# Weight blocks brought forward in a two-block mixer kernel, and the buffers rearranged for them

## The chip, the cores and the metric

The kernel runs on one core of a Trainium2 chip, as one program. The metric is the device time of an execution in microseconds. Three runs of the kernel before took 1659.3, 1660.58 and 1669.26 us; the median, 1660.58 us, is the time before.

## The reference, cut to what matters

Two blocks work on 256 latent tokens (and 256 context tokens in the first block) of width 1024, in float32. The first block has two layers:

```python
# layer 0 (context and latents), then layer 1 (latents only at the end)
mod = silu(c) @ mod_w[layer] + mod_b[layer]           # six vectors of 1024: sh1, sc1, g1, sh2, sc2, g2
h   = rmsnorm(x, norm_mix_g) * (1 + sc1) + sh1
y   = even_mixer(h)  (layer 0)   or   odd_mixer(h)  (layer 1)
x   = x + g1 * y
h   = rmsnorm(x, norm_ffn_g) * (1 + sc2) + sh2
x   = x + g2 * (silu(conv(h @ w_up)_g) * conv(h @ w_up)_a) @ w_down
```

`even_mixer` is a gated linear attention (4 heads) and an mLSTM (4 heads), both in two directions; their eight head outputs, 128 features each, go through `even_w_out` (1024 x 1024). `odd_mixer` is an SSD with 4 groups of 8 heads in two directions; the group outputs of 512 features are gated by silu(z), normalised per group and go through `ssd_w_out` (2048 x 1024). `w_up` is 1024 x 5632. The second block (attention, recurrence and gating branches) is not touched by the change.

## The kernel before, in words

Activations are kept with features on the 128 partitions. Every large weight is loaded as float32 in blocks of mostly 128 x 2048 (1 MB) and split in two halves of 16 bits: `get_w` (L318) asks SP for the load into a staging tile `st`, ScalarE casts it to `whi` (float16), and VectorE or GpSimd (`eng`) writes the rest, `wlo` = `st` - `whi` (bfloat16). A product then takes three matmuls per 128 x 128 weight tile, `whi` by the high half of the activations, `whi` by the low half, `wlo` by the high half (`proj_fm`, L328). The common staging pool `wst` and the common pool of halves `wsp` have three buffers each; `pool` and `parts` put the staging tile or the halves elsewhere.

The order of instructions on each engine isn't written out by hand: the program is traced in the order of the Python code, and a planner, which simulates the engines as it goes, places the instructions, earlier code first, later code where an engine would be free. What it placed runs in that order on every engine. A tile of a pool that reuses memory waits for the tiles that lay there.

- `layer0_mixer` (L538): gated linear attention, mLSTM inputs, the mLSTM heads one after another (`hd` 0 to 3, each ends with `hm` and is split into `h`). Then the tail: mod steps 2, 3 and 4 of layer 0 (`mod_steps`, four loads of 1 MB each, multiplied in float32 straight from staging), the four blocks of `even_o` (blocks 0 and 1 take the first four head outputs, 2 and 3 the last four), the products `eo` with their residual additions into `xT`, the norm of the context tokens and mod step 5. The blocks' halves are in the pool `tw` of four buffers. The products and the mod steps share two accumulators (`mm`).
- `ffn` (L972), called for layer 0 with both streams and for layer 1 with the latents. The 22 w_up blocks have their low part on GpSimd, those of odd number a staging pool of their own (`stage`). During the first FFN, the mod steps of layer 1 run as halves of 0.5 MB with pools `ms` and `mp` of two buffers, one half after each w_up block and the rest inside the down projection.
- `ssd` (L1083): for each group g, `inputs(g + 1)` is traced between the heads of group g (`heads`), and the output product of an earlier group (`out`) beside it; `take` advances these generators. `steps` prepares the decays once, with softplus. The output of the heads of all four groups is in `ys`, 16 tiles of 128 x 256 in two halves. For group 3 the scale `factor` is applied after the product: `ps` is multiplied by it (`so`) before the residual additions. In `out`, group g reads `ys` from 4g. At the end of `ssd` w_up blocks 0 and 1 of the second FFN are traced (`first_up`), in the common pools.
- `ffn` for layer 1 then norms the latents (`rstd_bc`: squares, a chain of additions `sq`, `rsqrt`; then `nt`, `hh`, `hl` per 128 features) and goes on with these two blocks.

Of the kernel before, what the change touches and what calls it, by code (L numbers as in the profile page):

```python
# [10 lines left out]
F32 = mybir.dt.float32  # L11
# [237 lines left out]
class Program:  # L249
# [288 lines left out]
    def layer0_mixer(self):  # L538
        h, I = self.h, self.I
        with ExitStack() as ph:  # L540
            gp = self.pool("gp", 1, None, ph)
            ev = self.pool("ev", 1, None, ph)
            mp = self.pool("mp", 1, None, ph)
            yf = ev.tile([128, 8, 512], F32, name="yf")
            mqk = ev.tile([128, 8, 512], F32, name="mqk")
            vext = ev.tile([128, 4, 4, 129], F32, name="vext")
            self.rows = [mp.tile([128, 512], F32, name=n) for n in ("li", "lf", "lb", "lm")]
            for t in self.rows:
                self.G.memset(t[:64], 0.0)
            self.G.memset(vext[:, :, :, 128:129], 1.0)  # L550
            self.gla(gp, h, I["even_w"], yf)
            self.mlstm_inputs(h, I["even_w"], mqk, vext, yf)
            for i in range(4):
                self.split(h[0][:, i], h[1][:, i], yf[:, i])
            self.mlstm(mp, h, mqk, vext, yf)
            self.dbg("ym", h[0])
        self.res2 = self.pool("res2")
        self.xT = self.res2.tile([128, 8, 512], F32, name="xT")
        self.nc.sync.dma_start(self.xT, I["xT"].rearrange("p (k t) -> p k t", k=8))
        with ExitStack() as tail:  # L560
            tw = self.pool("tw", 4, None, tail)
            for r in (2, 3, 4):
                for _ in self.mod_steps(0, r, whole=True):
                    pass
            w = [self.get_w(I["even_o"][b], 4, 512, parts=tw) for b in range(4)]

            for b in range(2):
                for c in range(4):
                    ps = self.mm("eo")
                    self.proj_fm(ps, w[b], c * 128, 128, h, 0, 512, nk=4)  # L570
                    self.add_residual(ps, 0, 2, 4 * b + c, BOTH)

            for s in range(2):
                for b in range(2):
                    for c2 in range(2):
                        ps = self.mm("eo")
                        for c in range(2):
                            self.proj_fm(ps[:, c * 256:c * 256 + 256], w[2 + b], (2 * c2 + c) * 128, 128, h,
                                         256 * s, 256 * s + 256, nk=4, h0=4)
                        for c in range(2):  # L580
                            self.add_residual(ps[:, c * 256:], 0, 2, 4 * b + 2 * c2 + c, ((s, 0, 256),), 256 * s)
                if s == 0:
                    self.norm_stream(0, 1, 0, "ml")
            for _ in self.mod_steps(0, 5, pool=tw, whole=True):
                pass
        self.dbg("xmid0", self.xT)
# [385 lines left out]
    def ffn(self, l, streams):  # L972
        I, V = self.I, self.V
        both = len(streams) == 2
        n, t0 = (512, 0) if both else (256, 256)
# [3 lines left out]
        if both:  # L979
# [3 lines left out]
            for i in range(3):  # L983
                w = self.get_w(I["w_up"][l, i], 8, 256, self.G)
# [21 lines left out]
        with ExitStack() as ph:  # L1006
            fp = self.pool("fp", 1, None, ph)
            f2 = self.pool("f2", 3, None, ph)
            stage = self.pool("stage", 1 if both else 3, None, ph)
# [1 line left out]
            self.nc.sync.dma_start(fcw, I["fcw"][l].rearrange("p (c j) -> p c j", c=44))  # L1011
            hid = self.pair(fp, "hid", [128, 22, n])
            if both:
                ms, mp = self.pool("ms", 2, None, ph), self.pool("mp", 2, None, ph)
                up = True
                mods = chain.from_iterable(self.mod_steps(1, r, eng=lambda: self.G if up else None, pool=ms, parts=mp,
                                                          halves=True) for r in range(6))
            for i in range(22):
                begun = both and i < 3
                if begun:  # L1020
                    w, pss = first[i]
                elif not both and i < 2:
                    w = self.first_up[i]
                else:
                    w = self.get_w(I["w_up"][l, i], 8, 256, self.G, (None, stage)[i % 2])
                us = []
                for c in range(2):
                    ps = pss[c] if begun else self.mm("up")
# [43 lines left out]

    def layer1_mixer(self):
        h, I = self.h, self.I
        with ExitStack() as ph:
            sp = self.pool("sp", 1, None, ph)
            s2 = self.pool("s2", 2, None, ph)
            y = self.pair(sp, "ys", [128, 16, 256])
            self.ssd(sp, s2, h, y)
            self.dbg("ys", y[0])  # L1080
        self.dbg("xmid1", self.xT[:, :, 256:512])

    def ssd(self, sp, s2, h, y):  # L1083
# [17 lines left out]
        def steps(ps):  # L1101


            t1 = lambda n: sp.tile([128, 256], F32, name=n)
            z, e, u, q, dt, cum = t1("z"), t1("e"), t1("u"), t1("q"), t1("dt"), t1("cum")
            self.ts(z, ps[:, :256], self.pp("sdtb"), op0=ALU.add)
            self.softplus(dt, z, e, u, q, 256)
            self.dbg("dt", dt)
# [58 lines left out]
        def out(g, factor=None):  # L1167

            for b in range(2):
                w = self.get_w(I["ssd_o"][2 * g + b], 4, 512)  # L1170
                for c in range(2):
                    ps = self.mm("so")
                    for cc in range(2):
                        self.proj_fm(ps[:, cc * 256:cc * 256 + 256], w, c * 256 + cc * 128, 128, y, 0, 256, nk=4, h0=4 * g)
                    if factor is not None:
                        t = s2.tile([128, 512], F32, tag="xs", name="so")
                        self.tt(t.rearrange("p (c t) -> p c t", c=2), ps.rearrange("p (c t) -> p c t", c=2), bc(factor, 1, 2), ALU.mult)
                        ps = t
# [18 lines left out]
        def inputs(g, d):  # L1197
# [32 lines left out]
            px = self.ps("fr", "bTT")  # L1230
            for t in range(4):
                T.transpose(px[:, t * 128:t * 128 + 128], bT[:, t * 128:t * 128 + 128], self.ident)
            bt = d["bt"] = s2.tile([128, 4, 128], F32, tag="bt", name="bt")
            self.act(bt, px.rearrange("p (a b) -> p a b", a=4))
            ps = self.ps("fr", "CB")
            for sb in range(2):
# [43 lines left out]
        def heads(g, D):  # L1280
# [3 lines left out]
            for j in range(4):  # L1284
# [41 lines left out]
                                 start=True, stop=True)  # L1326
                self.tt(yt[:, j], yt[:, j], Y[:, :256], ALU.add)
                self.tt(yt[:, j], yt[:, j], D["sz"][:, j], ALU.mult)
                sq = s2.tile([128, 256], F32, tag="ssq", name="ssq", bufs=4)
                self.act(sq, yt[:, j], AF.Square)  # L1330
                if j:
                    self.tt(sq, sq, sums, ALU.add)
                sums = sq
                if g == 3:
                    self.split(y[0][:, 12 + j], y[1][:, 12 + j], yt[:, j], scale=hg[:, 12 + j:13 + j])
            ps = self.ps("fr", "ss")
            for tb in range(2):
                T.matmul(ps[:, tb:tb + 1], sums[:, tb * 128:tb * 128 + 128], self.ones[:, 0:1], start=True, stop=True)
# [1 line left out]
            r = self.cols.tile([128, 2], F32, tag="sr", name="sr")  # L1340
            self.ts(v, ps[:, 0:2], 1.0 / 2048, EPS, ALU.mult, ALU.add)
            self.rsqrt(r, v, 2)
            dg = s2.tile([128, 2, 128], F32, tag="dg", name="dg")
            self.tt(dg, bc(self.ident, 1, 2), bc(r, 2, 128), ALU.mult)
            yield
            pb = self.ps("fr", "rb")
# [5 lines left out]
            for j in range(4):  # L1352
                k = 4 * g + j
                self.stt(yt[:, j], yt[:, j], hg[:, k:k + 1], pb[:, :256], ALU.mult, ALU.mult)
                self.split(y[0][:, k], y[1][:, k], yt[:, j])

        def take(it, n=1):
            for _ in range(n):
# [5 lines left out]
        for g in range(4):  # L1364
# [16 lines left out]
            take(now)  # L1381
            if g < 3:
                states(g + 1, nxt)
                nxt["factor"] = None
                D = nxt
            else:
                factor = D["factor"]
        take(out(3, factor), 99)

        self.first_up = [self.get_w(I["w_up"][1, i], 8, 256) for i in range(2)]  # L1390

    def softplus(self, o, z, e, u, q, n):

# [536 lines left out]
    def run(self):  # L1930
# [31 lines left out]
        self.layer1_mixer()  # L1962
        self.set_psum(mm=7, nb=1)
        self.ffn(1, ((1, 0, 256),))
        self.dbg("xend1", self.xT[:, :, 256:512])
        self.set_psum(mm=2, pT=1, av=1, x=1, sc=2, fl=1)
        self.block2()
# [27 lines left out]
```

## Time and profile before

| | |
|---|---|
| median of the runs | 1660.58 us (1659.3 to 1669.26) |
| the profiled execution | 1671.3 us, its span 1669.5 us |
| TensorE busy | 1579.9 us (95%) |
| VectorE busy | 1205.0 us (72%) |
| ScalarE busy | 848.8 us (51%) |
| GpSimd busy | 449.1 us (27%) |
| granted TensorE clock, mean | 0.972 |
| HBM read | 233.68 MB, 141 GB/s over the span |

Times in views of the trace are microseconds from the start of the span. PE is TensorE, PEld its weight loads, DVE VectorE, ACT ScalarE, POOL GpSimd, SP the engine that issues the loads (its rows show the issue, not the transfer). A row of the timeline gives start, duration, engine, line of the kernel (often that of a helper), operation, output and inputs, count, and in brackets the idle time of the engine before it with what ended it. The stages: first mixer to about 360, first FFN to 740, SSD to 1071, second FFN to 1270, then the second block.

### The profile page before, as it was taken

How to read it: one execution, taken by the hardware profiler on the slowest of the kernel's cores; microseconds unless marked ns; L12 is line 12 of the kernel's file. 1: busy time of each engine (PE TensorE's matmuls, PEld its weight loads, DVE VectorE, ACT ScalarE, POOL GpSimd, SP SyncE). 2: the span in 40 equal slices, each digit the busy share in tenths (PEclk: the TensorE clock that was granted, in tenths of full speed). 3: DMA queues.
4: the chain of work that ended last, by engine and by line, in shares of the span. 5: the costliest groups of instructions: out<-in, count | busy, mean ns of one | idle time of the engine just before them, and what ended most of it. 6: DMA issues, size and time to landing. Idle time of an engine off the chain costs nothing.

```text
span 1669.5 us, 31742 instructions
## 1 busy us (share of the span) xinstructions
PE 1579.9 (95%) x12913; PEld 1088.6 (65%) x12978; DVE 1205.0 (72%) x2636; ACT 848.8 (51%) x1390; POOL 449.1 (27%) x265
## 2 busy tenths in 40 slices
PE   6999999899999999998999999599999999999988
PEld 3566865477444444375566667488887887778877
DVE  6888745778777786556878888799967875366734
ACT  4746424435545544434566564366664644556532
POOL 0000000035878730000000000079944212421240
PEclk9999999899999999999999999799999989999999
DMA  9322126633443346632222323335454343433641
GB/s 388 106 80 77 53 77 255 262 145 114 152 151 126 119 160 211 200 115 76 101 76 77 126 76 131 153 132 201 150 184 163 139 164 107 147 114 124 231 158 51
DMA packets 41186, 236.77 MB, mean 142 GB/s; under 512 B 4688, under 2 KB 5456, under 8 KB 21200
## 3 DMA queue, kind: packets, MB, share of 16 engines
q1 hardware_dynamic: 41040, 234.74, 39.9%
q8 instruction: 102, 1.67, 0.4%
q14 instruction: 44, 0.36, 0.1%
HBM read 233.68 MB, written 1.05 MB: 141 GB/s over the span
## 4 chain that ended last, share of the span: by engine, by line
PE 75%; DVE 11%; ACT 5%; DMA 4%; issue 4%; POOL 1%; ACTq 0%; SPq 0%; DVEq 0%; POOLq 0%
PE up L332 18%; PE dn L332 5%; PE sx L332 5%; PE fm L332 4%; PE mg L332 4%; DVE wlo L294 3%; ACT whi L306 3%; DVE u L303 3%; PE br L332 3%; PE tm L339 3%; PE eo L332 2%; PE so L332 2%; PE sz L332 2%; DMA st<-in_mod_w_dram 2%; PE mod L505 2%
## 5 line engine op out<-in xcount | busy, mean ns | idle before, releaser
L332 PEld LDWEIGHTS <-whi 128*128 128x128 f16 (+2 forms) x5240 | 512.7, 99 | 259.4 <-issue 36.9
L294 POOL TENSOR_TENSOR wlo<-st,whi 128x1024 bf16<-128x1024 f32 (+2 forms) x102 | 315.2, 3102 | 964.4 <-ACT whi L306 651.8
L306 ACT ACTIVATE whi<-st 128x2048 f16<-128x2048 f32 (+3 forms) x242 | 370.0, 1538 | 266.4 <-PE up L332 45.4
L294 DVE TENSOR_TENSOR wlo<-st,whi 128x2048 bf16<-128x2048 f32 (+3 forms) x140 | 278.9, 1997 | 93.7 <-ACT whi L306 89.1
L332 PEld LDWEIGHTS <-wlo 128*128 128x128 bf16 (+2 forms) x2620 | 259.9, 99 | 125.9 <-issue 12.4
L303 DVE SCALAR_TENSOR_TENSOR u<-up,fcw,u 128x189 f32<-128x189 f32 (+3 forms) x792 | 297.8, 435 | 51.1 <-ACT u L306 42.8
L332 PE MATMUL up<-hh,whi 128*128 128x256 f16 (+1 forms) x752 | 238.5, 319 | 1.9 <-ACT hh L306 1.1
L332 PE MATMUL up<-hh,wlo 128*128 128x256 f16 (+1 forms) x752 | 238.3, 318 | 1.0
L332 PE MATMUL up<-hl,whi 128*128 128x256 bf16 (+1 forms) x733 | 231.2, 316 | 0.0
L332 PE MATMUL dn<-hidh,wlo 128*128 128x256 f16 (+1 forms) x396 | 122.4, 311 | 3.5 <-DVE wlo L294 2.7
L332 PE MATMUL dn<-hidh,whi 128*128 128x256 f16 (+1 forms) x396 | 122.3, 310 | 0.9 <-ACT whi L306 0.7
L332 PE MATMUL dn<-hidl,whi 128*128 128x256 bf16 (+1 forms) x384 | 117.8, 308 | 0.0
L306 ACT ACTIVATE u<-up,ppt,fcw 128x512 f32<-128x512 f32 (+1 forms) x88 | 57.9, 659 | 43.9 <-PE up L332 43.9
L332 PE MATMUL fm<-hh,whi 128*128 128x256 f16 x288 | 78.5, 273 | 0.5 <-DVE xc L303 0.5
L332 PE MATMUL fm<-hh,wlo 128*128 128x256 f16 x288 | 78.5, 273 | 0.0
L332 PE MATMUL fm<-hl,whi 128*128 128x256 bf16 x288 | 78.5, 273 | 0.0
L332 PE MATMUL mg<-hh,wlo 128*128 128x256 f16 x256 | 72.2, 282 | 3.1 <-POOL wlo L294 3.1
L332 PE MATMUL mg<-hh,whi 128*128 128x256 f16 x256 | 71.8, 282 | 2.1 <-ACT whi L306 1.2
L332 PE MATMUL mg<-hl,whi 128*128 128x256 bf16 x256 | 72.1, 282 | 1.2 <-DVE hl L303 1.2
L339 PEld LDWEIGHTS <-hh 128*128 128x128 f16 x640 | 62.9, 101 | 10.2 <-issue 1.1
L298 POOL TENSOR_SCALAR E<-E,rs 128x128 f32<-128x128 f32 (+1 forms) x48 | 37.1, 787 | 111.6 <-DVE rs L1669 51.1
L332 PE MATMUL sx<-hh,wlo 128*128 128x512 f16 (+1 forms) x160 | 53.3, 336 | 0.4
(539 smaller groups left out, 3043.6 us busy)
## 6 DMA issues: line engine op xcount, KB each, us to landing
st<-in_w_up_dram SPq DMA_DIRECT2D x44, 1024.0 KB, 4.9
st<-in_w_dram SPq DMA_DIRECT2D x25, 1024.0 KB, 4.8
st<-in_mod_w_dram SPq DMA_DIRECT2D x48, 512.0 KB, 4.6
st<-in_w_dn_dram SPq DMA_DIRECT2D x32, 704.0 KB, 4.1
st<-in_ssd_w_dram SPq DMA_DIRECT2D x20, 1024.0 KB, 4.9
st<-in_mod_w_dram SPq DMA_DIRECT2D x16, 1024.0 KB, 5.7
st<-in_w_m_dram SPq DMA_DIRECT2D x32, 512.0 KB, 4.4
st<-in_even_w_dram SPq DMA_DIRECT2D x14, 1024.0 KB, 4.9
```

The costliest lines, as they stand in the source:

```text
L294: (eng or self.V).tensor_tensor(o, a, b, op=op)
L298: (eng or self.V).tensor_scalar(o, a, s1, None, op0=op0)
L303: self.V.scalar_tensor_tensor(o, a, s, b, op0=op0, op1=op1)
L306: self.S.activation(o, i, func, **kw)
L332: self.T.matmul(ps, w[a][:, k, c0:c0 + cw], h[b][:, h0 + k, t0:t1], start=first and k == 0 and i == 0, stop=last and k == nk - 1 and i == 2)
L339: self.T.matmul(ps, h[b][:, k, t0:t0 + 128], w[a][:, k, c0:c0 + cw], start=k == 0 and i == 0, stop=k == nk - 1 and i == 2)
L505: T.matmul(ps[32 * j:32 * j + 32, :256], c[:, 2 * b + k], w[:, 0 if halves else k, 256 * j:256 * j + 256], start=b == k == i == 0, stop=b ...
```

## The change

It moves loads and splits, gives some of them other buffers, and makes room for these buffers.

- Layer 0 tail: `even_o` blocks 0 and 1 are traced ahead of the mod steps, in the common pools; blocks 2 and 3 stay behind them in `tw`, which has two buffers now. Mod step 5, which stages in `tw`, has two buffers too.
- First FFN: three buffers for the mod halves.
- Second FFN: block 2's low part goes to VectorE; GpSimd has it from block 3 on.
- Blocks 0 and 1 of the second FFN have halves in a pool `fu` of their own, and are traced after the states of group 3, ahead of group 3's heads, its remaining inputs and the last two output products. `fu` lives until the second FFN is over.
- For the 16 KB of `fu`: `ys` has 8 tiles (groups g and g + 2 share), softplus's z, e, u, q lie in the buffers of `E` and `wx`, `bt` and `dg` have one buffer, `ssq` three.

```diff
@@ layer0_mixer
-            tw = self.pool("tw", 4, None, tail)
+            tw = self.pool("tw", 2, None, tail)
+            w = [self.get_w(I["even_o"][b], 4, 512) for b in range(2)]
             for r in (2, 3, 4):
                 for _ in self.mod_steps(0, r, whole=True):
                     pass
-            w = [self.get_w(I["even_o"][b], 4, 512, parts=tw) for b in range(4)]
+            w += [self.get_w(I["even_o"][b], 4, 512, parts=tw) for b in (2, 3)]
@@ ffn
-                ms, mp = self.pool("ms", 2, None, ph), self.pool("mp", 2, None, ph)
+                ms, mp = self.pool("ms", 3, None, ph), self.pool("mp", 3, None, ph)
...
-                    w = self.get_w(I["w_up"][l, i], 8, 256, self.G, (None, stage)[i % 2])
+                    w = self.get_w(I["w_up"][l, i], 8, 256, self.G if both or i > 2 else None, (None, stage)[i % 2])
@@ layer1_mixer
+        self.fu_stack = self.ctx.enter_context(ExitStack())
         with ExitStack() as ph:
+            self.fu = self.pool("fu", 2, None, self.fu_stack)
...
-            y = self.pair(sp, "ys", [128, 16, 256])
+            y = self.pair(sp, "ys", [128, 8, 256])
@@ ssd
-            z, e, u, q, dt, cum = t1("z"), t1("e"), t1("u"), t1("q"), t1("dt"), t1("cum")
+            dt, cum = t1("dt"), t1("cum")
+            z, e, u, q = [s2.tile([128, 512], F32, tag=n, name=n)[:, 256 * i:256 * i + 256] for n in ("E", "wx") for i in (0,)
+                          for _ in range(2)]
...
-                        self.proj_fm(ps[:, cc * 256:cc * 256 + 256], w, c * 256 + cc * 128, 128, y, 0, 256, nk=4, h0=4 * g)
+                        self.proj_fm(ps[:, cc * 256:cc * 256 + 256], w, c * 256 + cc * 128, 128, y, 0, 256, nk=4, h0=4 * g % 8)
...
-            bt = d["bt"] = s2.tile([128, 4, 128], F32, tag="bt", name="bt")
+            bt = d["bt"] = s2.tile([128, 4, 128], F32, tag="bt", name="bt", bufs=1)
...
-                sq = s2.tile([128, 256], F32, tag="ssq", name="ssq", bufs=4)
+                sq = s2.tile([128, 256], F32, tag="ssq", name="ssq", bufs=3)
...
-                    self.split(y[0][:, 12 + j], y[1][:, 12 + j], yt[:, j], scale=hg[:, 12 + j:13 + j])
+                    self.split(y[0][:, 4 + j], y[1][:, 4 + j], yt[:, j], scale=hg[:, 12 + j:13 + j])
...
-            dg = s2.tile([128, 2, 128], F32, tag="dg", name="dg")
+            dg = s2.tile([128, 2, 128], F32, tag="dg", name="dg", bufs=1)
...
-                self.split(y[0][:, k], y[1][:, k], yt[:, j])
+                self.split(y[0][:, k % 8], y[1][:, k % 8], yt[:, j])
...
             if g < 3:
                 states(g + 1, nxt)
-                nxt["factor"] = None
                 D = nxt
-            else:
+            if g == 2:
+                self.first_up = [self.get_w(I["w_up"][1, i], 8, 256, parts=self.fu) for i in range(2)]
+            if g == 3:
                 factor = D["factor"]
         take(out(3, factor), 99)
-
-        self.first_up = [self.get_w(I["w_up"][1, i], 8, 256) for i in range(2)]
@@ run
         self.ffn(1, ((1, 0, 256),))
+        self.fu_stack.close()
```

## Rows read from the trace of the kernel before

**Rows 1.** The profile's busy times: us, share of the span, instructions.

```profile
PE 1579.9 (95%) x12913; PEld 1088.6 (65%) x12978; DVE 1205.0 (72%) x2636; ACT 848.8 (51%) x1390; POOL 449.1 (27%) x265
```

**Rows 2.** Windows: length, each engine's busy us (count), clock, DMA share, GB/s.

```profile
225.00:255.00 30.00, 29.79 (x152) 14.38 (x151) 14.72 (x41) 7.78 (x19) 0.00 (x0) 1.00 0.10 35
300.00:311.00 11.00, 7.61 (x42) 7.07 (x40) 7.29 (x33) 3.61 (x11) 0.00 (x0) 0.69 0.01 1
311.00:315.30 4.30, 0.98 (x3) 0.31 (x4) 3.98 (x10) 4.30 (x4) 0.00 (x0) 0.84 0.87 295
315.30:328.30 13.00, 12.95 (x49) 5.66 (x51) 8.91 (x18) 3.33 (x3) 0.00 (x0) 0.79 1.01 422
```

**Rows 3.** SP's timeline, end of the first mixer.

```profile
250.81 28.58 SPq L315 DMA_DIRECT2D st<-in_mod_w_dram  x9
282.58 13.53 SPq L315 DMA_DIRECT2D st<-in_even_o_dram  x3
```

**Rows 4.** Timeline of ScalarE and VectorE, end of the first mixer.

```profile
311.08 5.50 ACT L306 ACTIVATE whi<-st 128x2048 f16<-128x2048 f32 x3
313.00 2.29 DVE L294 TENSOR_TENSOR wlo<-st,whi 128x2048 bf16<-128x2048 f32 x1
```

**Rows 5.** Windows, one stretch in the first FFN's down projection.

```profile
660.00:700.00 40.00, 38.24 (x235) 15.93 (x240) 22.50 (x25) 17.86 (x19) 0.00 (x0) 1.00 0.65 208
```

**Rows 6.** Windows, end of the SSD to the second FFN.

```profile
1033.00:1084.00 51.00, 30.45 (x205) 23.25 (x204) 39.07 (x87) 15.97 (x32) 4.06 (x1) 0.78 0.40 149
```

**Rows 7.** ScalarE's timeline, end of the SSD.

```profile
1037.31 1.91 ACT L306 ACTIVATE whi<-st 128x2048 f16<-128x2048 f32 x1 [5.28 <-issue]
1057.89 1.91 ACT L306 ACTIVATE whi<-st 128x2048 f16<-128x2048 f32 x1 [3.83 <-issue]
1059.71 0.37 ACT L306 ACTIVATE factor<-rb 128x256 f32<-128x256 f32 x1
```

**Rows 8.** Timeline of TensorE and VectorE around factor.

```profile
1057.75 0.67 PE L1347 MATMUL rb<-dg,ones 128*128 128x256 f32 x2
1059.83 2.29 DVE L294 TENSOR_TENSOR wlo<-st,whi 128x2048 bf16<-128x2048 f32 x1 [2.17 <-ACT whi L306]
1062.04 1.28 DVE L294 TENSOR_TENSOR so<-so,factor 128x512 f32<-128x512 f32 x2
1062.78 0.40 PE L332 MATMUL so<-ysh,whi 128*128 128x256 f16 x1 [4.37 <-DVE so L294]
```

**Rows 9.** The tile sq (ns: min, median, max); GpSimd's timeline; the norm.

```profile
L294 DVE TENSOR_TENSOR sq<-sq,s x7: 418/426/4078, 1064.8 to 1077.2; 128x256 f32<-128x256 f32 x7
...
1072.79 4.06 POOL L294 TENSOR_TENSOR wlo<-st,whi 128x2048 bf16<-128x2048 f32 x1 [448.44 <-ACT whi L306]
```

**Rows 10.** SP's timeline, SSD to second FFN.

```profile
984.62 26.79 SPq L315 DMA_DIRECT2D st<-in_ssd_o_dram  x4
1017.20 45.29 SPq L315 DMA_DIRECT2D st<-in_w_up_dram  x5
1070.90 0.33 SPq L1011 DMA_DIRECT2D fcw<-in_fcw_dram  x1
```

**Rows 11.** Windows, two stretches in the SSD.

```profile
945.00:960.00 15.00, 14.95 (x79) 8.05 (x78) 13.16 (x26) 6.11 (x12) 0.00 (x0) 1.00 0.40 140
985.00:1000.00 15.00, 14.95 (x125) 11.06 (x125) 14.06 (x30) 9.40 (x19) 0.00 (x0) 1.00 0.41 141
```

**Rows 12.** The chain of waits (start, us); ScalarE's timeline; SSD.

```profile
994.77 2.73 PE so L332 x24
...
1043.84 0.49 ACT L306 ACTIVATE ysh<-yt,hsg 128x256 f16<-128x256 f32 x1
```

**Rows 13.** The tile bt: ns min, median, max; first and last start.

```profile
L306 ACT ACTIVATE bt<-bTT x2: 597/624/652, 944.6 to 1010.6; 128x512 f32<-128x512 f32 x2
```

**Rows 14.** The profile's loads: count, KB each, us to landing.

```profile
st<-in_w_up_dram SPq DMA_DIRECT2D x44, 1024.0 KB, 4.9
```

**Rows 15.** The tile hl in the norm before the second FFN.

```profile
L303 DVE SCALAR_TENSOR_TENSOR hl<-nt,modc,hh x8: 482/484/485, 1084.0 to 1090.0; 128x256 bf16<-128x256 f32 x8
```

## The prediction

> **What bounds the kernel now.** I read the busy times first: TensorE is busy 1579.9 us of a span of 1669.5, so some 90 us are all that better order can win, less what a higher clock gives [rows 1]. Then I took windows over each stage that the diff touches, to see where those 90 us lie, and the queues and timelines inside the windows that had idle time.
>
> The first place is the end of the first mixer. TensorE is full from 225 to 255, but from 300 to 315.3 it idles 3.39 and 3.32 us, and the granted clock falls to 0.69 there and is still 0.79 up to 328.3: for part of that time it stands at the lower of its two levels (1.2 of 2.4 GHz) after the idle time [rows 2]. What ends the idleness is a weight split. The output blocks are queued behind the mod blocks [rows 3], and their casts sit in ScalarE's queue behind the last head's work: three casts begin at 311.08, the low part of the first follows at 313.00, though three of the blocks were asked for by 296 [rows 4].
>
> The second place is the end of the down projection of the first FFN. The chain of waits names mod-weight loads there, but TensorE is busy 38.24 of 40 us [rows 5]: the chain names a cover, not a bound.
>
> The third is the end of the SSD: from 1033 to 1084 TensorE is busy 30.45 of 51 us at a granted clock of 0.78 [rows 6]. ScalarE has two casts there (1037.31 and 1057.89) for which it first stood still 5.28 and 3.83 us, and `factor`, ready to be copied, comes out behind the second at 1059.71 [rows 7]. VectorE does the low part (2.29 us), only then the multiplication by `factor` at 1062.04, and TensorE, which waited 4.37 us, goes on at 1062.78 [rows 8]. Last, the norm before the second FFN: one addition `sq` takes 4.078 us instead of 0.418, while GpSimd has the low part of the third w_up block (1072.79, 4.06 us) [rows 9].
>
> To know which cast is which I counted loads: four ssd_o, then five w_up (blocks 0, 1, 2, 4, 6), then the staged ones [rows 10]. With three weight slots, the casts at 1037.31 and 1057.89 and the one in front of GpSimd's split at 1072.79 are w_up 0, 1 and 2; each waited until the block three earlier had left its slot.
>
> **The change, part by part.** The sum is made against the profiled execution, 1671.3 us with a span of 1669.5; the median of the runs is 1660.58, 10.7 us below it. I carry the difference over to the median unchanged.
>
> *Output blocks 0 and 1 first (A).* Two 1 MB loads pass twelve mod loads on SP's queue. DMA is nearly free from 225 to 255 (share 0.10), so the mods lose nothing [rows 2]. The two splits (ScalarE 2 x 1.8, VectorE 2 x 2.29) move from 311 into that stretch, where VectorE is busy 14.72 of 30 us and ScalarE 7.78: hidden; without that cover they'd cost 8.2. The matmuls of these blocks need only the first half of the mixer's output, which is ready, so they can fill TensorE's holes. Lower end: 0, if the planner still places them after the last head. Upper end: 3.39 + 3.32 us of idle time, and 13.0 x 0.21 = 2.7 us for the clock, 9.4 together. I take **8.0**: nearer the upper end, since TensorE has nothing else to do in these holes; the 1.4 left is my estimate for accumulators, of which there are two, waiting for their residual additions. The last mod step of layer 0 has two buffers instead of four, and two of its loads wait for its first matmuls; its result is wanted only by the down projection, past 600, so 0. The first w_up splits of the first FFN now need slots that blocks 0 and 1 hold: 0, as these are gone before the norm; without that cover 4.06 us, one GpSimd split [rows 9].
>
> *Three buffers for the mod halves (B).* Ends: 0, and the idle 40 - 38.24 = 1.76 us [rows 5]. I take **0.5**, since most of the stretch is matmuls back to back.
>
> *w_up 0 and 1 in slots of their own, split during the SSD (C1).* Two loads now pass sw18, sw19 and four ssd_o loads on SP. Their splits, 2 x 1.91 and 2 x 2.29, go to about 945 to 1000; TensorE is full there, VectorE at 13.16 and 14.06 of 15 us [rows 11]. I cost them 0 under TensorE; if VectorE sets the pace they cost 4.6. At the old place the second cast vanishes in front of `factor`: VectorE could multiply about when `factor` could be out, and the stretch from TensorE's last `so` to 1062.78 loses one cast and what it holds up. Without cast and low part, `factor` waits only for its matmul (1057.75 and 0.67) and takes 0.37 itself: some 1058.9 with the handovers, instead of the 1062.04 at which VectorE could multiply, **3.1 us** won [rows 7, 8]. Ends: 0 (another cast takes the place; more than one has no free slot) and 3.83 (the whole stall). The first cast (1037.31) I price at 0: w_up 2 inherits its slot and place, with its split on VectorE as that of w_up 0 was. If nothing took its place, 2.3 more.
>
> *w_up 2's low part on VectorE (C2).* GpSimd's 4.06 us at 1072.79 go, and with them the 4.078 - 0.418 = 3.66 us that `sq` stood [rows 9]. But GpSimd keeps blocks 3 and up, and w_up 4, loaded early through the common staging, can be cast as soon as a slot is free, at the end of the SSD, where w_up 2's was. Ends: +3.66 and, if blocks 3 and 4 both hit the norm, -3.66. I take **0**: w_up 4 is loaded and the third slot comes free at the same moment as before.
>
> *Room made for it.* y of two groups: the first write for group 3 comes at 1043.84, the matmuls of out(1), which read the reused half, are over by 997.5 (994.77 and 2.73) [rows 12]: 0. One bt: the copy at 1010.6 waits for state matmuls of the group before, and that group's own copy was at 944.6, so there are 66 us between [rows 13]: 0. One dg, three ssq, and softplus's four temporaries inside E and wx come in program order after their last readers: 0 each; if ScalarE did wait for one, the P and E casts queue behind it, by at most one such copy of 0.65 us a group. The fcw load and the FFN's buffers lie 16 KB higher; staged loads still go after 1070.9 [rows 10]: 0. The second FFN is not touched inside and moves as a block.
>
> Sum: 8.0 + 0.5 + 3.1 + 0 = **11.6 us faster**: 1659.7 for a run like the profiled one, 1649.0 at the median.
>
> **The port of VectorE and GpSimd.** The row shows it: 4.078 us against 0.418 for the same addition, next to GpSimd's split [rows 9]. The Trainium skill, "SBUF — State Buffer", section "Who interferes with whom", says that a VectorE instruction with two SBUF inputs and a GpSimd one that reads SBUF exclude each other for a whole instruction. By that rule moving one split wins nothing where others stay on GpSimd beside such instructions, and the page speaks against pricing C2 as won. The trace agrees for `sq`.
>
> **The rivals.**
>
> *All of it comes (chance 0.25).* Holes of A filled (9.4), both casts out of the way (3.1 + 2.3), `sq` free (3.66), B 1.76: 20.2 us, **1640**; with the 2.4 us that the clock of 0.69 costs in 300 to 311 (7.61 x 0.31), 1638. For it: nothing else needs TensorE in those holes. Against: w_up 2 and w_up 4 want the same slots.
>
> *The stall changes hands (0.25).* Block 3 is staged after 1070.9, lands 4.9 us later [rows 14], and has a slot now where it had to wait for w_up 0's. Its GpSimd split of 4.06 then lies on the norm's `hl`, eight instructions from 1084.0 to 1090.0 with two SBUF inputs [rows 15], and w_up 4's on `sq`: C2 becomes -3.66 and eats C1. With A at its lower half, 3 to 4, the sum is 3.5 us, **1657**. The same number comes if the planner leaves the output blocks behind the last head, so that part A doesn't do what it says: 0.5 + 3.1. The skill's rule above makes this case; what speaks against is that the order of the casts isn't fixed.
>
> *Slower (0.10).* ScalarE and VectorE work through their queues in order. If a split brought forward stands in ScalarE's queue before its load has landed, the E and P work behind it waits: 4.9 us a load [rows 14], and 2.29 on a VectorE that has 1 to 2 us free in 15 [rows 11]. For the two w_up blocks that is 2 x 7.2 = 14.4 us, **1675** if it takes A's and C's gain too. It decides once SP issues these loads later than the casts are planned; the last loads went out some 20 us ahead of their casts (1017.20 against 1037.31), which speaks against it.
>
> **How the numbers follow.** The forecast has a chance of 0.40, its own range 1642 to 1656. Changes within 1%, 16.6 us, are what a measurement of this kernel can't tell from none. Faster by more: most of "all of it" (0.22) and the upper edge of the forecast (0.08), 0.30. Slower by more: 0.05. The rest, 0.65, is within. The range 1636 to 1662 takes in "all of it" and "changes hands" and leaves out the slower case.
>
> **What would show it.** A: no idle time of TensorE over 1 us from 300 to 315, granted clock near 1, output matmuls before the last `hm`. C1: `factor` right behind its matmul, one w_up cast before 1063 instead of two. C2: a GpSimd split still beside `sq` or `hl`, or none. B: under 1 us. I am wrong if output matmuls still start after the last head, if TensorE idles in 945 to 1000, or if the norm before the second FFN shortens by 3.6 us.

## The result, and the profile after

The changed kernel took 1646.58 us at the median (1641.43 to 1650.74, 4 runs), the kernel before 1663.48 us on the same chip (4 runs): a ratio of 0.9895, interval 0.985 to 0.9939. That is 16.9 us faster. The forecast was 1649.0, its sum 11.6 us, its range 1636 to 1662; it was counted from 1660.58, the median of the three runs known then. The profiled execution of the changed kernel took 1646.4 us, its span 1644.6.

The page's busy times and the windows, to be read beside [rows 1, 2, 5, 6, 11] (length, then each engine's busy us and count in the order of the page, clock, DMA share, GB/s):

```profile
PE 1563.6 (95%) x12978; PEld 1083.6 (66%) x12978; DVE 1212.3 (74%) x2637; ACT 847.9 (52%) x1390; POOL 444.8 (27%) x264
```
```profile
225.00:255.00 30.00, 30.00 (x142) 15.05 (x141) 20.06 (x46) 11.84 (x22) 0.00 (x0) 1.00 0.36 140
300.00:311.00 11.00, 11.00 (x71) 7.24 (x70) 7.71 (x33) 3.53 (x8) 4.07 (x1) 1.00 0.31 101
311.00:315.30 4.30, 4.30 (x23) 2.22 (x22) 3.36 (x11) 2.83 (x4) 0.00 (x0) 1.00 0.88 373
315.30:328.30 13.00, 8.18 (x32) 3.19 (x31) 12.82 (x18) 4.15 (x3) 5.62 (x1) 0.90 0.93 337
356.00:367.00 11.00, 6.04 (x47) 3.20 (x44) 7.68 (x24) 3.85 (x9) 0.00 (x0) 0.67 0.57 210
660.00:700.00 40.00, 40.00 (x261) 18.27 (x260) 20.93 (x22) 15.95 (x17) 0.00 (x0) 1.00 0.56 181
945.00:960.00 15.00, 15.00 (x72) 7.12 (x71) 14.21 (x22) 10.28 (x18) 0.00 (x0) 1.00 0.62 211
985.00:1000.00 15.00, 15.00 (x133) 12.74 (x132) 11.03 (x25) 11.06 (x23) 0.00 (x0) 1.00 0.39 138
1017.00:1068.00 51.00, 33.60 (x230) 26.16 (x228) 38.43 (x88) 16.57 (x32) 7.92 (x2) 0.80 0.35 126
```

From 300 to 315.3, where TensorE idled 6.7 us before, it is full at clock 1.00. But two new holes stand behind: from 315.3 to 328.3 (8.18 busy of 13; 12.95 before) and from 356 to 367 (6.04 busy of 11, clock 0.67). In 660 to 700 the busy time rises only from 38.24 to 40, but the weight loads, one to each matmul, rise from 240 to 260: a twelfth more work in the same time. (The matmuls' own counts, 235 and 261, can't be compared as they stand: 65 of the 12978 matmuls of the kernel before have no record.) TensorE stays full where the two w_up splits went (945 to 1000). The last window lies 16 us earlier than that of [rows 6], which leads up to the second FFN, and has 33.60 busy of 51 for 30.45; the last `so` starts 19.5 us earlier (1051.1 for 1070.6).

The first of the new holes is VectorE's and GpSimd's. Before, GpSimd had its first split of a w_up block of the first FFN behind the last mLSTM head:

```profile
330.73 12.29 POOL L294 TENSOR_TENSOR wlo<-st,whi 128x2048 bf16<-128x2048 f32 x4 [293.87 <-PE eo L332]
```

In the changed kernel such a split runs beside that head's norm. GpSimd, VectorE and TensorE in turn:

```profile
318.95 5.62 POOL L294 TENSOR_TENSOR wlo<-st,whi 128x2048 bf16<-128x2048 f32 x1 [9.33 <-ACT whi L306]
```
```profile
320.57 4.02 DVE L303 SCALAR_TENSOR_TENSOR r<-rt,r 128x4 f32<-128x4 f32 x1
324.51 0.86 DVE L303 SCALAR_TENSOR_TENSOR xT<-eo,modc,xT 128x256 f32<-128x256 f32 x2
```
```profile
325.43 0.39 PE L332 MATMUL eo<-hh,whi 128*128 128x512 f16 x1 [4.15 <-DVE xT L303]
```

`r`, an instruction on 128 x 4 values that took 0.15 to 0.17 us at this place before, takes 4.02, until the split is through (318.95 + 5.62). The residual addition into `xT` stands behind it on VectorE, and TensorE waits for that addition to get an accumulator back. a_only, a_tw4 and tw4 show the same wait (4.15 to 4.16 us); in t5 the split falls on other instructions and the longest such wait is 1.73 us.

Where the time went is easiest to see by stages, measured in one profile of each kernel between the first or last starts of named matmuls (the views by tile). In us: mixer, from the last `gqk` (an input product of the gated linear attention) to the last `eo`; up, to the first `dn` (norm, mod step 5, up projection; `dn` is the down projection); dn, to the last mod matmul of the first FFN; SSD, to the last `so`; ffn2, to the last `up`; rest, to the end of the span. "before, again" is a second profile, told of below.

| kernel | mixer | up | dn | SSD | ffn2 | rest |
|---|---|---|---|---|---|---|
| before | 294.7 | 247.5 | 95.9 | 365.8 | 132.4 | 466.5 |
| before, again | 292.5 | 247.6 | 94.2 | 364.0 | 132.4 | 456.8 |
| changed | 285.9 | 253.3 | 87.5 | 356.3 | 133.1 | 460.4 |
| a_only | 285.7 | 253.4 | 96.9 | 361.5 | 132.4 | 457.2 |
| a_tw4 | 284.3 | 248.5 | 95.3 | 361.2 | 131.7 | 453.3 |
| b_only | 291.2 | 247.6 | 87.4 | 365.3 | 132.4 | 456.8 |
| b_stage | 292.7 | 247.5 | 92.3 | 365.9 | 132.4 | 453.5 |
| b_halves | 292.1 | 248.4 | 95.3 | 365.8 | 132.4 | 457.0 |
| c_only | 289.8 | 247.5 | 96.7 | 360.2 | 133.4 | 460.2 |
| t5 | 286.3 | 247.5 | 87.4 | 352.2 | 133.1 | 457.9 |
| tw4 | 287.6 | 248.4 | 87.4 | 357.5 | 132.9 | 464.0 |
| t5d4 | 293.7 | 247.6 | 87.4 | 352.8 | 133.0 | 458.7 |
| t5late | 288.6 | 247.5 | 87.4 | 354.0 | 135.4 | 454.6 |
| g2 | 283.9 | 253.1 | 87.4 | 358.6 | 133.6 | 459.9 |

The kernels' names are those of the experiments. One profile has a spread of its own: t5 and t5d4 run the same instructions up to the end of the SSD, and their mixer differs by 7.4 us (t5d4 had a granted clock of 0.95 to 0.97 in parts of it). The column dn repeats to 0.1 us between the seven kernels with part B whole. The last stage of the first profile of before is 10 us longer than in its second, and that of tw4 6 us longer than that of t5; that is no part of the change.

### The profile page after: what moved, and what is told of

It is laid out like the page before. It is cut to its first block, busy times and chain, and to the rows that moved or that the text cites. A ratio compares the mean times of both kernels' runs of the same rounds, so it can differ in the third digit from the quotient of the medians.

```text
span 1644.6 us, 31809 instructions
## 1 busy us (share of the span) xinstructions
PE 1563.6 (95%) x12978; PEld 1083.6 (66%) x12978; DVE 1212.3 (74%) x2637; ACT 847.9 (52%) x1390; POOL 444.8 (27%) x264
## 4 chain that ended last, share of the span: by engine, by line
PE 81%; DVE 8%; ACT 4%; DMA 3%; issue 3%; POOL 1%; ACTq 0%; SPq 0%; DVEq 0%; POOLq 0%
PE up L332 19%; PE dn L332 9%; PE sx L332 5%; PE fm L332 4%; PE mg L332 4%; PE br L332 3%; PE mqk L332 2%; PE tm L339 2%; ACT whi L306 2%; PE so L332 2%; DVE wlo L294 2%; PE mod L505 2%; PE sz L332 2%; DVE u L303 2%; PE sc L1664 2%
## 5 line engine op out<-in xcount | busy, mean ns | idle before, releaser
L332 PEld LDWEIGHTS <-whi 128*128 128x128 f16 (+2 forms) x5240 | 511.5, 99 | 253.3 <-issue 38.1
L294 POOL TENSOR_TENSOR wlo<-st,whi 128x2048 bf16<-128x2048 f32 (+2 forms) x101 | 311.7, 3097 | 935.5 <-ACT whi L306 934.8
L306 ACT ACTIVATE whi<-st 128x2048 f16<-128x2048 f32 (+3 forms) x242 | 369.1, 1536 | 253.3 <-PE dn L332 46.6
L294 DVE TENSOR_TENSOR wlo<-st,whi 128x2048 bf16<-128x2048 f32 (+4 forms) x141 | 279.0, 1988 | 83.8 <-ACT whi L306 82.1
L332 PE MATMUL up<-hl,whi 128*128 128x256 bf16 (+1 forms) x752 | 238.1, 317 | 2.0 <-DVE hl L303 1.9
L332 PE MATMUL dn<-hidl,whi 128*128 128x256 bf16 (+1 forms) x396 | 122.5, 310 | 0.0
L294 POOL TENSOR_TENSOR sg<-sg,u 128x512 f32<-128x512 f32 (+1 forms) x44 | 44.2, 1004 | 45.6 <-ACT sg L306 45.3
```

Of the source, the lines that this page charges most:

```text
L294: (eng or self.V).tensor_tensor(o, a, b, op=op)
L306: self.S.activation(o, i, func, **kw)
L332: self.T.matmul(ps, w[a][:, k, c0:c0 + cw], h[b][:, h0 + k, t0:t1], start=first and k == 0 and i == 0, stop=last and k == nk - 1 and i == 2)
```

## The experiments

**a_only, b_only, c_only: one part each, on the kernel before.** a_only has the output blocks' order with `tw` at two buffers, b_only three buffers for the mod halves, c_only all that concerns the second FFN's blocks.

```diff
 a_only  -tw = self.pool("tw", 4, None, tail)   +tw = self.pool("tw", 2, None, tail)   +w = [... for b in range(2)] ahead
 b_only  -ms, mp = ... 2 ... 2   +ms, mp = ... 3 ... 3
 c_only  +self.fu ..., first_up after states, "i > 2", ys [128, 8, 256], ...
```

> The kernel before with part A alone: output blocks 0 and 1 ahead of the mod steps, two buffers in tw. Theory 1 (holes filled, then given back): the last eo product ends some 9 us earlier against the start of the stage, but mod step 5, staged in two buffers, makes TensorE wait some 5 to 7 us for its last two loads, so that the first FFN begins only 2 to 4 us earlier; time about 3 us under the kernel before (ratio 0.998). Theory 2 (the forecast's term): 8 us, ratio 0.995, no wait for the mod loads.

> The kernel before with part B alone: three buffers for the mod halves. Theory 1 (each switch of TensorE between dn and a mod half costs some 0.1 us that the busy time hides, and three halves in a row share a switch): the stretch from the first dn product to the last mod row is 8 us shorter, ratio about 0.995. Theory 2 (the forecast's term): at most 1.8 us, ratio 0.999 to 1.000; the 8 us between the two profiles were the spread of executions.

> The kernel before with everything but A and B: w_up 0 and 1 in their own buffers and split during the SSD, the room made for it, w_up 2's low part on VectorE. Theory 1: from the start of the SSD to the second FFN some 8 us are won, 2 of them in the tail and the rest because the SSD's instructions are placed otherwise; ratio 0.995. Theory 2 (the forecast's terms): 3.1 us in the tail and nothing ahead of it, ratio 0.998. In both, one addition sq of 4 us is gone and two instructions hl take over 6 us together beside GpSimd.

Measured (before: 1664.19): a_only 1659.86, ratio 0.998 [0.9959, 1.0001]; b_only 1658.11, 0.9972 [0.995, 0.9993]; c_only 1659.74, 0.9981 [0.9962, 1.0]. So A, the largest term of the forecast, can't be told from the others, and B, the smallest, is the only one whose interval leaves out no change. The three alone add up to 11.2 us (3.3, 4.7 and 3.2) for the 16.9 together; each is uncertain by some 3.5, so that the difference says nothing. a_only came as theory 1 has it, and so did the stage of b_only, though not its whole (4.7 us for 8); c_only has the ratio of theory 2, and the two `hl` of 6.38 us that both had foretold. The table says how: A wins 4 to 9 us in the mixer (285.7 against 289.8 to 294.7 in the kernels without it) and loses 5.8 in the next stage; B wins 6.8 to 8.5 in dn; C and A each shorten the SSD by 2.5 to 5.6.

**t5: the changed kernel with staging of its own for mod step 5.**

```diff
+            t5 = self.pool("t5", 4, None, tail)
-            for _ in self.mod_steps(0, 5, pool=tw, whole=True):
+            for _ in self.mod_steps(0, 5, pool=t5, whole=True):
```

> The changed kernel with four staging buffers again for mod step 5 (a pool of its own; tw keeps two). Theory 1 (two buffers make TensorE wait for mod 5's loads): the DMA wait of about 6.8 us ahead of the last mod matmuls goes, the first FFN starts 4 to 6 us earlier, ratio to the kernel before about 0.986. Theory 2 (the norm's chain on VectorE sets the start of the first FFN anyway): no change against the changed kernel, ratio 0.989.

Measured: 1636.14, ratio 0.9836 [0.9813, 0.9858]. The stage "up" is back at 247.5, which is 5.8 of the 10.2 us between the two profiles; 4.1 more lie in the SSD (352.2 for 356.3), where the two kernels don't have the same order of instructions. The reason for the 5.8 stands in TensorE's timeline of the changed kernel (start, duration, count, and the idle time before with its releaser) and in SP's:

```profile
354.17 1.93 PE L505 MATMUL mod<-st,cs 128*32 128x256 f32 x32
360.25 1.93 PE L505 MATMUL mod<-st,cs 128*32 128x256 f32 x16 [4.15 <-DMA st<-in_mod_w_dram]
363.00 1.93 PE L505 MATMUL mod<-st,cs 128*32 128x256 f32 x16 [0.81 <-DMA st<-in_mod_w_dram]
```
```profile
341.53 14.96 SPq L315 DMA_DIRECT2D st<-in_mod_w_dram  x4
356.54 0.43 SPq L1012 DMA_DIRECT2D fcw<-in_fcw_dram  x1
```

The last two loads of the step leave SP only when the first two blocks have been multiplied, and TensorE, which works in order, stands before them with the norm's and the up projection's matmuls queued behind. In t5 the same 64 matmuls run in one piece:

```profile
356.49 3.66 PE L505 MATMUL mod<-st,cs 128*32 128x256 f32 x64
```

**a_tw4 and tw4: `tw` at four buffers again**, in a_only and in the changed kernel.

```diff
-            tw = self.pool("tw", 2, None, tail)
+            tw = self.pool("tw", 4, None, tail)
```

> The kernel before with part A's order alone: output blocks 0 and 1 ahead of the mod steps, tw kept at four buffers, so that mod step 5 has its four too. Theory: A's order wins the 7 to 9 us that it wins up to the last output product, and what the kernel with all of A gave back was the wait of mod step 5 behind two buffers; this kernel then starts its first FFN 5 to 9 us earlier, about 1657, ratio 0.995 to 0.9965. Rival: the order's gain is lost between the output product and the FFN anyway, ratio 0.998 as with all of A.

> The changed kernel with tw at four buffers again. Theory: only mod step 5 needs them, and this kernel takes what the one with four buffers of their own for that step takes, 1636, ratio about 0.984. Rival: the common pool is what slows it, since the last output blocks then split ahead of mod step 5 again, and it stays near 1646.

Measured (before: 1663.03): a_tw4 1656.32, ratio 0.9948 [0.9922, 0.9974]; tw4 1644.86, 0.9882 [0.9853, 0.991]. The order alone is worth 8.6 us [4.3 to 13.0], and its stage "up" is 248.5 where a_only has 253.4: the theory holds for part A. (The row of a_tw4 in the table is of its fastest run, 1645.51.) For tw4 the theory's time (1636) did not come and the rival's (near 1646) did, but not for the rival's reason: tw4 has the gain in "up" too (248.4). What it lacks is elsewhere: its SSD takes 357.5 us, that of t5 352.2, and TensorE's order there isn't the same. Why the planner's two orders differ by that, no run here shows.

**b_stage and b_halves: which of B's buffers.** The kernel before with three staging buffers and two for the halves, and the other way round. TensorE's order isn't the same in the two, as the expectations take it to be. From the first `dn` on, counted by the order of the weight loads, the mod matmuls stand in 41 runs in the kernel before, in 33 in b_stage, in 13 in b_halves and in 12 in b_only.

```diff
 b_stage   +ms, mp = self.pool("ms", 3, None, ph), self.pool("mp", 2, None, ph)
 b_halves  +ms, mp = self.pool("ms", 2, None, ph), self.pool("mp", 3, None, ph)
```

> The kernel before with three staging buffers for the mod halves, their split halves still in two. Two theories for what part B won (first FFN's down projection 95.9 us in the kernel before, 87.4 with three of both). Theory 1, the order: in the program before, TensorE turns from the down projection to mod matmuls 40 times, mostly for one group of four, and each turn costs some 0.3 us that busy time doesn't show; with one more buffer of either sort the mod matmuls stand in 16 runs, so this kernel wins the same: stage 87 to 89 us, ratio about 0.997. Theory 2, the loads: the casts waited 32.3 us for mod loads, and a third staging buffer takes that wait away: the same 87 to 89 us here, and nothing for the other kernel, the one with three buffers for the split halves alone.

> The kernel before with three buffers for the split mod halves, staging still in two. Its order on TensorE is that of the kernel with three staging buffers, instruction by instruction. Theory 1, the order: stage 87 to 89 us, ratio about 0.997. Theory 2, the loads: the third staging buffer is missing, so the casts still wait for loads and the stage stays near 96 us, ratio about 1.0.

Measured (before: 1665.36): b_stage 1657.76, ratio 0.9951 [0.9932, 0.997]; b_halves 1663.89, 0.9997 [0.9978, 1.0016]. b_halves has the better order and wins nothing: the order alone is not enough, and theory 1 falls as it stands. b_stage wins, but in its trace dn shortens to 92.3 only, not to the 87 to 89 of theory 2; it takes both buffers for 87.4. (The whole of b_stage is 8.2 us faster [5.0 to 11.3], more than its stage, and that of b_only 4.7 [1.2 to 8.3], less than its stage: wholes that differ by 3 us can't be ranked here.) The chain of waits over the stage tells the kernels apart (shares of it; 610 to 700 of before, b_halves and b_stage, 610 to 696 of b_only, in this order):

```profile
by line: PE dn L332 35.3%; DMA st<-in_mod_w_dram 33.6%; ACT whi L306 11.1%; DVE wlo L294 9.9%; issue 4.1%; PE mod L505 3.9%; DVE xT L303 1.0%; DVE sq L294 0.5%; PE mod L514 0.4%; ACTq L306 0.3%; DVEq L294 0.1%
```
```profile
by line: DMA st<-in_mod_w_dram 38.0%; PE dn L332 25.9%; ACT whi L306 12.3%; DVE wlo L294 11.8%; issue 6.6%; PE mod L505 2.9%; DVE sq L294 0.9%; DVE xT L303 0.7%; PE mod L514 0.4%; ACTq L306 0.3%; PE up L332 0.2%; DVEq L294 0.2%
```
```profile
by line: PE dn L332 88.7%; PE mod L505 10.3%; PE mod L514 1.4%
```
```profile
by line: PE dn L332 91.2%; PE mod L505 7.8%; PE mod L514 1.2%
```

With two staging buffers, load, cast and low part follow one another through the whole stage. One round of it in the kernel before, from the pieces of its chain:

```profile
648.90 5.89 DMA st<-in_mod_w_dram
...
654.90 1.07 ACT whi L306
...
655.99 1.24 DVE wlo L294
...
657.24 5.04 DMA st<-in_mod_w_dram
```

A buffer is given back 8.3 us after its load was asked for (648.90 to 657.24); two buffers make one half every 4.2 us. At that rate 95.9 us are 23 halves; the code leaves 26 of its 48 to the down projection, some of them loaded before it begins. The third staging buffer breaks that ring. What is left in b_stage shows in the waits (engine, releaser: us, times, longest), first of before, then of b_stage, then of b_only:

```profile
ACT whi L306 <- DMA st<-in_mod_w_dram: 32.3, 14, 4.8
PEld L505 <- issue: 17.1, 42, 0.5
```
```profile
ACT whi L306 <- PE mod L505: 15.6, 6, 3.8
PEld L505 <- issue: 13.4, 32, 0.4
```
```profile
PEld L505 <- issue: 4.9, 12, 0.4
ACT whi L306 <- DMA st<-in_mod_w_dram: 4.3, 3, 3.7
```

b_stage's casts no longer wait for loads but for TensorE to give back a half's slot, and its order still turns to a mod group 33 times; the weight loads stand idle before 32 of them, 0.42 us each, with both buffers before 12. So two limits lie close together: the ring, with which b_halves takes 95.3 us in spite of its good order (at a granted clock of 0.98 there, 1.00 in the kernel before), and the turns, with which b_stage takes 92.3 without the ring. That the remaining 4.9 us (92.3 to 87.4) are the turns is worked out in the last section; no run changes the order alone once the ring is gone.

**g2 and t5d4: the low parts of w_up blocks 2 to 4.** g2 is the changed kernel with block 2's low part on GpSimd again, t5d4 is t5 with those of blocks 3 and 4 on VectorE too.

```diff
 g2    -self.G if both or i > 2 else None   +self.G
 t5d4  -self.G if both or i > 2 else None   +self.G if both or i > 4 else None
```

> The changed kernel with part C2 undone: block 2's low part on GpSimd again. The forecast priced C2 at 0, because the lock changes hands: hl is held by the splits of blocks 3 and 4 as before, block 2's split falls some 30 us earlier, beside the last heads. Then this kernel takes what the changed one takes, 1646 within 3 us, and sq takes 0.42 us in it as well. Rival: C2 is worth the 3.66 us that sq stood in the kernel before: sq is held for 4 us again, and the time is about 1650.

> The changed kernel with four staging buffers for mod step 5, and the low parts of the second FFN's blocks 3 and 4 on VectorE too. Theory: in the changed kernel GpSimd's two splits (8.27 us) hold the norm's first two hl (6.39 us where two take 0.97); without them hl takes 0.48 each, but the two splits stand on VectorE ahead of hl, 2 x 2.29 us: 5.4 won, 4.6 paid, so 0 to 2 us faster than with the staging buffers alone (1636.1), about 1635. Rival: hl waits for something else (its hh or the clock), then VectorE's 4.6 us come on top, about 1641.

Measured (before: 1665.36): g2 1651.06, ratio 0.9924 [0.9892, 0.9955]; t5d4 1641.41, 0.9853 [0.9826, 0.988]. Neither can be told from the kernel it was made from by the ratios, though both medians came nearer to the rivals' times (1650 and 1641) than to the theories' (1646 and 1635). The rivals' reasons aren't in the traces: in g2 `sq` takes 0.426 us at most, as in the changed kernel, and in t5d4 the stage ffn2 is not longer. So it wasn't block 2's new engine that freed `sq`: the split had moved away with its block (in g2 GpSimd has it at 1022.79, and the norm begins past 1048). What stands in the norm now is the splits of blocks 3 and 4. The changed kernel, ScalarE, GpSimd and VectorE in turn:

```profile
1044.80 0.38 ACT L306 ACTIVATE factor<-rb 128x256 f32<-128x256 f32 x1 [5.97 <-PE rb L1353]
...
1058.09 3.71 ACT L306 ACTIVATE whi<-st 128x2048 f16<-128x2048 f32 x2 [4.30 <-DMA st<-in_w_up_dram]
1061.71 0.89 ACT L306 ACTIVATE hh<-nt,modc 128x256 f16<-128x256 f32 x2
```
```profile
1060.08 8.27 POOL L294 TENSOR_TENSOR wlo<-st,whi 128x2048 bf16<-128x2048 f32 x2 [437.08 <-ACT whi L306]
```
```profile
1045.21 1.29 DVE L294 TENSOR_TENSOR so<-so,factor 128x512 f32<-128x512 f32 x2 [2.45 <-ACT factor L306]
...
1062.23 6.39 DVE L303 SCALAR_TENSOR_TENSOR hl<-nt,modc,hh 128x256 bf16<-128x256 f32 x2 [2.05 <-ACT hh L306]
```

Two `hl` take 6.39 us, until GpSimd is through (1060.08 + 8.27). In t5d4 GpSimd does nothing there, and `hl` is short, but behind two splits on VectorE:

```profile
1058.83 2.29 DVE L294 TENSOR_TENSOR wlo<-st,whi 128x2048 bf16<-128x2048 f32 x1 [1.78 <-ACT whi L306]
...
1061.83 2.28 DVE L294 TENSOR_TENSOR wlo<-st,whi 128x2048 bf16<-128x2048 f32 x1
1064.03 0.87 DVE L303 SCALAR_TENSOR_TENSOR hl<-nt,modc,hh 128x256 bf16<-128x256 f32 x2
```

The stage ffn2 is 133.0 us for 133.1 in t5: won and paid back. The profile of t5d4 is 7.1 us longer than that of t5, and its mixer, where both have the same instructions, 7.4.

**t5late: blocks 3 and 4 into the slots of `fu`**, on t5.

```diff
-... (None, stage)[i % 2])
+... (None, stage)[i % 2], self.fu if not both and i in (3, 4) else None)
```

> The changed kernel with four staging buffers for mod step 5, and the halves of the second FFN's blocks 3 and 4 in the two slots of fu, which come free when blocks 0 and 1 have been multiplied. Theory: their two GpSimd splits no longer stand beside the first hl, but blocks 5 and 6 find the common slots free instead and stand there: the lock changes hands once more, and the time is 1636 within 3 us. Rival: the norm is free of splits and the 5.4 us come, 1631.

Measured: 1638.95, ratio 0.985 [0.982, 0.9881]. The theory holds: GpSimd has two splits at that place again, and `hl` stands beside them:

```profile
1059.44 8.28 POOL L294 TENSOR_TENSOR wlo<-st,whi 128x2048 bf16<-128x2048 f32 x2 [437.08 <-ACT whi L306]
```
```profile
1059.80 3.99 DVE L303 SCALAR_TENSOR_TENSOR hl<-nt,modc,hh 128x256 bf16<-128x256 f32 x1 [1.38 <-ACT hh L306]
...
1064.22 4.17 DVE L303 SCALAR_TENSOR_TENSOR hl<-nt,modc,hh 128x256 bf16<-128x256 f32 x2
```

**before2: the kernel before, again.**

> The kernel before, unchanged, profiled a second time. In its first profile the second block (last down projection to the end of the span) takes 402.6 us and in every other kernel's 394 to 396, with the same instructions. Theory: that is the spread of one execution (that profile was 7.8 us over the median of its runs), and this one shows 394 to 396. Rival: the second block follows from the stages ahead of it, and this one shows 402 again. The ratio to itself, 1.000, shows what a measurement makes of no change.

Measured: 1660.46, ratio to itself 0.999 [0.9969, 1.001]; last down projection to the end 395.4 us. The theory holds: the 402.6 of the first profile were its own. The other kernels show 392.1 to 400.6 (tw4) there, a wider spread than the 394 to 396 that the expectation names.

## Why the prediction was right in its total, and where its steps were not

The time came within 2.4 us of the forecast and the gain within 5.3 (16.9 for 11.6), and that closeness is in good part luck, errors that cancel: one wait of A priced at nothing and another too low, B far too small, the SSD's own gain not in the sum. The 2.4 us are also counted from a kernel before of 1660.58, which was 1663.48 in the measurement.

**A, 8.0.** The size of the term came: a_tw4, the order with nothing else, is 8.6 us faster [4.3 to 13.0], though 2.8 to 4.6 of the profile's gain lie in the SSD, where the term has nothing. The signs named came, too: TensorE full from 300 to 315, the first `eo` at 293.1 instead of 313.0. But 1.4 us were set aside for accumulators that wait for their residual additions, and these waits take 4.8 (0.67 and 4.15) right behind 315: the forecast asked only whether the first w_up splits of the FFN would find their slots in time, and these splits came earlier than before, beside the head's norm. The step that failed outright is "the last mod step of layer 0 has two buffers instead of four ... its result is wanted only by the down projection, past 600, so 0". I asked when the result is wanted, and not what stands behind the waiting instruction on TensorE's queue. It cost 5.8 us ("up", 253.3 for 247.5), and A as made is worth 3.3 by a_only.

**B, 0.5, at most 1.76.** Here the step failed that set the size: "the chain names a cover, not a bound". The chain of waits was right. I took the bound of the gain from the idle time of TensorE, 1.76 of 40 us, but a busy TensorE was doing 240 weight loads with their matmuls in the time of 260. Measured: 6.8 to 8.5 us of the stage, 4.7 [1.2 to 8.3] of the whole.

**C1, 3.1.** The second cast is gone from in front of `factor`, which now waits for `rb` alone (5.97 <- PE rb); the first (5.28 <- issue before a cast at 1021.14) stayed for w_up 2, as priced. What that is worth shows in TensorE's wait behind the first multiplication by `factor`. It was 4.37 us [rows 8]; the changed kernel:

```profile
1045.95 0.27 PE L332 MATMUL so<-ysh,whi 128*128 128x256 f16 x1 [1.20 <-DVE so L294]
```

It is 1.20 us in all seven kernels that have these two blocks' splits in the SSD, c_only among them, and 4.37 to 4.44 in the kernels without: 3.2 us less for the term's 3.1. c_only's SSD is 3.8 to 5.6 us shorter, its whole 3.2 [0 to 6.3]; what its SSD wins beyond `factor` isn't explained.

**C2, 0.** Right, and for the reason of the rival "the stall changes hands": ffn2 is 0.7 us longer in the changed kernel. (The forecast's lower end, -3.66 us, was priced for just this case, that blocks 3 and 4 both hit the norm.) `sq` lost its stall [rows 9] and `hl`, 0.48 us each before [rows 15], took it over, by blocks 3 and 4 both. The rival had the place right and its total (1657) wrong, for A and B came.

The rule of the Trainium skill, "SBUF — State Buffer", section "Who interferes with whom", agrees with the trace in three kernels: `hl`, an instruction with two SBUF inputs, lasts until GpSimd's split ends in the changed kernel and t5late, and takes 0.486 us at most where GpSimd is idle (t5d4). `r` with its 4.02 us at the end of the mixer agrees as well.

**What no step foresaw.** The SSD itself is shorter with A alone, by 2.5 to 4.6 us (a_only, a_tw4), where nothing of A lies. The SSD's instructions stand in another order there than in the kernel before, while b_only keeps the order of before and has an SSD of 365.3, no shorter. That the order makes the difference is argued from this; no run changes it alone. Of the changed kernel's 7.7 to 9.5 us there, C has 3.8 to 5.6 by c_only. It could not be read from the trace of before.

**The slower case** did not come: TensorE is full from 945 to 1000, and the one cast brought forward that met its load late waited 0.79 us.

## What to carry to other kernels

Before an engine's waiting instruction is priced at nothing, ask who stands behind it in that engine's queue; when its result is wanted doesn't matter. A stage in which TensorE is 96% busy can still be bound by a ring of load, split and buffer: where the chain of waits names the ring, divide its length by its buffers and compare with the stage, and compare counts of weight loads in equal times, not busy shares. Two limits can lie so close together that lifting one alone shows little (b_stage) or nothing (b_halves). Where VectorE and GpSimd shut each other out, moving one instruction away doesn't free the place while others queue for it; and when a sign such as "no idle time from 300 to 315" has come, look right behind the window, too.

The version with staging of its own for mod step 5 (t5) beats both kernels: 1636.14 us, ratio 0.9836 [0.9813, 0.9858] to the kernel before.

## What the runs showed that I had not expected

A group of four mod matmuls costs TensorE more when it stands alone among those of the down projection than in a row of such groups. The kernel before (start, duration):

```profile
639.85 0.38 PE L332 MATMUL dn<-hidl,whi 128*128 128x512 bf16 x1
640.16 0.29 PE L505 MATMUL mod<-whi,c 128*32 128x256 f16 x4
640.38 0.39 PE L332 MATMUL dn<-hidh,wlo 128*128 128x512 f16 x1
640.61 0.38 PE L332 MATMUL dn<-hidh,whi 128*128 128x512 f16 x1
```

From `dn` to `dn` over the group it is 0.53 us, where `dn` follows `dn` in 0.22. In the changed kernel six such groups begin at 647.06 to 647.61, 0.11 us apart:

```profile
646.75 0.38 PE L332 MATMUL dn<-hidh,wlo 128*128 128x512 f16 x1
647.06 0.29 PE L505 MATMUL mod<-whi,c 128*32 128x256 f16 x4
...
647.61 0.28 PE L505 MATMUL mod<-wlo,c 128*32 128x256 bf16 x4
647.83 0.39 PE L332 MATMUL dn<-hidh,whi 128*128 128x512 f16 x1
```

So each turn to the mod matmuls and back costs 0.53 - 0.22 - 0.11 = 0.2 us, and the 21 turns that b_stage has over b_only some 4 of their 4.9 us. That is an estimate from these two places. The busy time shows nothing of it, since each row of a matmul (0.38 us) is longer than the step to the next.
